# Ten feed-forward blocks by seven products, with the weight sums of two of them formed ahead and kept in DRAM

## The chip, the core and the metric

The kernel runs on one core of one Trainium2 chip. The metric is the device time of one execution in microseconds. A core has a matrix engine (TensorE, PE in the profile; its weight loads are listed as PEld), three engines for elementwise work (VectorE or DVE, ScalarE or ACT, GpSimd or POOL) and SyncE (SP), which here only issues transfers. Each engine works through its own instruction list in order and waits on semaphores. Sixteen DMA engines move data between DRAM and the core's memory; a transfer belongs to the queue of the engine that issued it. Sums of products build up in eight banks of PSUM, each 128 partitions by 512 floats.

## The reference

Two layers work on 256 tokens of width 2048, all in float32. Cut to what matters:

```python
for l in range(DEPTH):                        # 2
    h = rms_norm(x, norm1_g[l])
    z = h @ w_in[l]                           # 2048 x 3584
    mixed = ...                               # gated unit and windowed attention on parts of z
    x = x + mixed @ w_out[l]                  # 2048 x 2048
    h2 = rms_norm(x, norm2_g[l])
    x = x + (jax.nn.silu(h2 @ w_gate[l]) * (h2 @ w_up[l])) @ w_down[l]   # 2048 x 5632, 5632 x 2048
```

The change is about the last line, and about what runs beside the projections ahead of it.

## The kernel before

**Three products for one.** TensorE multiplies in a short float format (`float32r`). Each operand is split into a high part and a rest; `mm3` (lines 133 to 136) adds three matmuls: high times high, high times rest, rest times high. Activations are split once. Weights are split as they come in: `raw_load` brings a tile of 128 x 2 x 512 floats (512 KB, buffer `raw`, 7 of them) through SP's queue, and `split2` makes `wh` with a copy on ACT (line 95, 5 buffers) and `wl` with a subtraction on DVE (line 96, 4 buffers).

**A unit** is one such tile with its 12 matmuls of 128 x 512 (two halves, two groups of 128 tokens, three products). After a unit `tick()` counts a clock on, and actions entered by `later(delay, fn)` are emitted when their tick has come. In this way small steps are laid between units of matmuls in program order. The scheduler of the language then orders instructions by that order and by free buffers.

**The first part of a layer** consists of 7 blocks of 8 units (`in_block`, columns 6, 4, 5, 2, 3, 0, 1 of `w_in`), with the attention's steps placed at ticks (`UNIT_AT`), and of the output projection, 8 parts of 4 units (`add_part`). In attention DVE, ACT and POOL normalize, form the softmax and split the results; POOL computes the inverse roots (`inv_rms`, line 182, with the name `ir`) and issues the loads of the bias (line 317).

**The feed-forward part** has 11 column blocks of 512. For blocks in `GU_BLOCKS` (0 and 1), `gate_up` multiplies gate and up in the ordinary way, 16 units. For blocks in `S_BLOCKS` (2 to 10), `seven` uses a scheme like Strassen's: taking the two token groups, two interleaved halves of the depth, and the gate and up columns as 2 x 2 matrices, it needs 7 products in place of 8. A product runs through four rounds `i`, each a half-unit of 6 matmuls, so 28 half-units a block. Five PSUM banks `m0` to `m4` hold the products. In a round of the first phase DVE forms three sums of weight tiles: `b11 + b12` (line 605), that plus `b22` into `t2` (line 606), and `b12 + b22` (line 611). An accumulating transfer on POOL's queue (line 613) adds the fourth weight tile onto `t2`, which is kept for the second phase. After the first phase DVE combines the banks (lines 624 to 629); the second phase adds the products of `b21` to bank `m0` and those of the kept sums to bank `m2`, whose result DVE adds once more (line 638), and then come the SiLU on ACT (line 641) and the product with it on DVE (line 643).

**The mixture.** `s_stream` yields after each half-unit of `seven`. `std_stream` yields ordinary units: those of `gate_up`, and those of `down`, which multiplies by `w_down` two or three finished blocks at a time. Finished blocks are transposed and split by `act_T` (line 555) into tiles with the tag `aT`, of which there are 8. How many ordinary units follow a half-unit is set by `debt`, a running balance of DVE's cost (`VEC`, `VEC_P`) against PE's (`MM` times `LOAD`): ordinary units are emitted while the balance is positive. What is left runs after the last block.

Of the kernel before, what the change touches and what calls it, by code (L numbers as in the profile page):

```python
# [12 lines left out]
F32 = mybir.dt.float32  # L13
# [3 lines left out]
ALU = mybir.AluOpType  # L17
AX = mybir.AxisListType
PSUM = bass.MemoryType.PSUM

P = 128
D = 2048
SEQ = 256
NTOK = SEQ // P
# [16 lines left out]
ND = D // NB  # L41
S_BLOCKS = (2, 3, 4, 5, 6, 7, 8, 9, 10)
GU_BLOCKS = tuple(b for b in range(NFF) if b not in S_BLOCKS)
CHUNK = (2, 3)
ACT_TILES = 8
VEC = 1.14
VEC_P = 0.6
MM = 0.227
LOAD = 0.93
WARM = 12  # L50
# [14 lines left out]
def trunk(ctx, tc, x, xt, w_in, w_out, w_gate, w_up, w_down, sgu_w, sgu_g, consts,  # L65
# [7 lines left out]
    ap = ctx.enter_context(tc.tile_pool(name="ap", bufs=2))  # L73
    sp = ctx.enter_context(tc.tile_pool(name="sp", bufs=4))
    pa = ctx.enter_context(tc.tile_pool(name="pa", bufs=5, space=PSUM))
    pd = ctx.enter_context(tc.tile_pool(name="pd", bufs=2, space=PSUM))
# [12 lines left out]
    def split2(raw):  # L89
        wh = wp.tile([P, 2, NB], F32R, tag="wh", name="wh", bufs=5)  # L90
        wl = wp.tile([P, 2, NB], F32R, tag="wl", name="wl", bufs=4)
        step = 2 if clock[0] > 1 else 1
        for j in range(0, 2, step):
            src = raw[:, j : j + step, :]
            nc.scalar.copy(wh[:, j : j + step, :], src)  # L95
            nc.vector.tensor_tensor(  # L96
                wl[:, j : j + step, :], src, f(wh[:, j : j + step, :]), ALU.subtract
            )
        vec(1)
        return wh, wl  # L100

    clock = [0]
    debt = [0.0]

    def vec(n, cost=VEC):
        debt[0] += n * cost

    def pe(n):
        debt[0] -= n * MM * LOAD

    serial = itertools.count()
# [26 lines left out]
    def unit(src, acts, acc, first, last, again=False):  # L138
        raw = raw_load(src, 2 if clock[0] < 4 else 1)
        wh, wl = split2(raw)  # L140
        for j in range(2):
            act, aj = acts[j]
            for t in range(NTOK):
# [4 lines left out]
                )  # L148
        pe(12)
        tick()  # L150
# [100 lines left out]
    for lay in range(L):  # L251
# [226 lines left out]
        def norm_block(n, ss, pairs, lay, col, ext=None):  # L478
# [11 lines left out]
            for t in range(NTOK):  # L490
                sum_sq(ss[:, t, n : n + 1], xres[:, t, n * NB : (n + 1) * NB])

        acc_kv = in_block(6)
        if lay == 0:
# [55 lines left out]
        def act_T(b, c, sg, pairs_f=pairs_f):  # L550
# [4 lines left out]
            nc.vector.tensor_tensor(pair[:, 1], ps, f(pair[:, 0]), ALU.subtract)  # L555
            vec(1, VEC_P)
            pe(2)
            pairs_f.setdefault(b, []).append(pair)
# [16 lines left out]

        def seven(b, lay=lay, pairs2=pairs2, ext2=ext2, act_later=act_later):
            bank = [pa.tile([P, NB], F32, tag="acc", name=f"m{i}") for i in range(5)]

            def s_unit(raw, m, i, op, first, last, bank=bank):
                wh, wl = split2(raw)  # L580
                for j in range(2):
# [4 lines left out]
                    )  # L586
                pe(6)
                tick(0.5)
# [6 lines left out]

            kept = []
            for i in range(4):
                b11 = raw_load(w_gate[lay, b, i, 0])
                b12 = raw_load(w_up[lay, b, i, 0])
                b22 = raw_load(w_up[lay, b, i, 1])  # L600
                t2 = ap.tile([P, 2, NB], F32, tag="spt", name="t2", bufs=4)
                first, last = i == 0, i == 3
                s_unit(b11, 0, i, a_op(0, 0), first, last)
                yield
                nc.vector.tensor_tensor(b11, b11, b12, ALU.add)  # L605
                nc.vector.tensor_tensor(t2, b11, b22, ALU.add)
                s_unit(b11, 1, i, e_op(1), first, last)
                vec(1)
                vec(1)
                yield  # L610
                nc.vector.tensor_tensor(b12, b12, b22, ALU.add)
                s_unit(t2, 3, i, e_op(2), first, last)
                nc.gpsimd.dma_start(t2, w_gate[lay, b, i, 1], accum_op=ALU.add)  # L613
                vec(1)
                yield
# [8 lines left out]
            nc.scalar.copy(m0, bank[0])  # L624
            nc.vector.tensor_tensor(m0, bank[3], m0, ALU.add)
            nc.vector.tensor_tensor(c12, bank[1], m0, ALU.add)
            nc.vector.tensor_tensor(c12, bank[4], c12, ALU.add)
            nc.vector.tensor_tensor(c21, bank[2], m0, ALU.add)
            nc.vector.tensor_tensor(c22, bank[1], c21, ALU.add)
            vec(5, VEC_P)  # L630
            yield
            for i in range(4):
                b21 = raw_load(w_gate[lay, b, i, 1])
                s_unit(b21, 0, i, a_op(1, 0), False, i == 3)
                yield
                s_unit(kept[i], 2, i, a_op(1, 1), False, i == 3)
                yield
            nc.vector.tensor_tensor(m0, bank[2], m0, ALU.add)
            sg = [zp.tile([P, NB], F32, tag="z", name="sg0"), m0]
            for t, c in ((0, bank[0]), (1, m0)):  # L640
                nc.scalar.activation(sg[t], c, AF.Silu, scale=rstd2[t])
            for t, c in ((0, c12), (1, c22)):
                nc.vector.scalar_tensor_tensor(sg[t], c, nrstd2[t], sg[t], ALU.mult, ALU.mult)
            vec(3, VEC_P)
            act_later(b, sg)
# [17 lines left out]
        def gate_up(b, even=even, act_later=act_later):  # L663
# [7 lines left out]
            for t in range(NTOK):  # L671
                nc.vector.scalar_tensor_tensor(
                    sg[t], acc[t], rstd2[t], sg[t], ALU.mult, ALU.mult
                )
            vec(NTOK, VEC_P)
            act_later(b, sg)
# [49 lines left out]
        other = std_stream()  # L726
        debt[0] = 0.0
        for _ in s_stream():
            while debt[0] > 0.0 and next(other, False):
                pass  # L730
        seven_done[0] = True
# [93 lines left out]
```

## Time and profile before

| quantity | value |
|---|---|
| median of 3 runs | 1953.2 us (1952.04 to 1955.46) |
| profiled execution | 1952.96 us, span 1951.2 us |
| granted TensorE clock | 0.999 |
| PE busy | 1936.5 us, 99% |
| DVE busy | 1624.8 us, 83% |
| ACT busy | 1253.2 us, 64% |
| POOL busy | 115.3 us, 6% |
| moved by DMA | 422.2 MB, 216 GB/s on the mean |

The profile is one execution, and its busy times are unions: two instructions of an engine that overlap count once. The first 270 us are layer 0's projections, attention and output projection, the feed-forward part runs to about 900 us, and layer 1 repeats both. A matmul's duration in a row is the time from its start to its modelled end, so neighbours overlap. In rows of groups, "idle before" is how long the engine stood idle ahead of these instructions, with what ended that idling.

### The profile page before, as it was taken

How to read it: one execution, taken by the hardware profiler on the slowest of the kernel's cores; microseconds unless marked ns; L12 is line 12 of the kernel's file. 1: busy time of each engine (PE TensorE's matmuls, PEld its weight loads, DVE VectorE, ACT ScalarE, POOL GpSimd, SP SyncE). 2: the span in 40 equal slices, each digit the busy share in tenths (PEclk: the TensorE clock that was granted, in tenths of full speed). 3: DMA queues.
4: the chain of work that ended last, by engine and by line, in shares of the span. 5: the costliest groups of instructions: out<-in, count | busy, mean ns of one | idle time of the engine just before them, and what ended most of it. 6: DMA issues, size and time to landing. Idle time of an engine off the chain costs nothing.

```text
span 1951.2 us, 24946 instructions
## 1 busy us (share of the span) xinstructions
PE 1936.5 (99%) x8884; PEld 1587.5 (81%) x8884; DVE 1624.8 (83%) x1712; ACT 1253.2 (64%) x1651; POOL 115.3 (6%) x116
## 2 busy tenths in 40 slices
PE   9999999999999999999999999999999999999999
PEld 6788888888888888888887888888888888888887
DVE  6566689999999999999556656899999999999983
ACT  7565566666666666667756755666656666666674
POOL 1210000000000000000002000000000000000000
PEclk9999999999999999999999999999999999999999
DMA  9544557768678678768555355586686787778773
GB/s 358 192 146 153 189 169 227 231 225 264 214 218 268 210 229 254 226 215 262 193 200 192 132 164 181 174 256 214 214 274 205 230 253 228 221 233 247 226 252 116
DMA packets 117804, 422.20 MB, mean 216 GB/s; under 512 B 13104, under 2 KB 13744, under 8 KB 117680
## 3 DMA queue, kind: packets, MB, share of 16 engines
q1 hardware_dynamic: 105264, 375.52, 55.2%
q0 software_dynamic: 12416, 45.09, 12.8%
q8 instruction: 69, 1.13, 0.2%
q14 instruction: 55, 0.45, 0.1%
HBM read 418.47 MB, written 2.10 MB: 216 GB/s over the span
## 4 chain that ended last, share of the span: by engine, by line
PE 91%; DVE 3%; issue 3%; ACT 1%; DMA 1%; POOL 1%; SPq 0%; ACTq 0%; DVEq 0%; POOLq 0%
PE m L135 11%; PE m L136 11%; PE m L134 11%; PE dacc L135 10%; PE dacc L134 10%; PE dacc L136 10%; PE acc L135 8%; PE acc L136 8%; PE acc L134 8%; DVE wl L96 1%; PE ps_f L199 1%; POOL ir L182 1%; PE ps_v L372 1%; PE ps_n L199 1%; ACT s L349 0%
## 5 line engine op out<-in xcount | busy, mean ns | idle before, releaser
L95 ACT CAST wh<-raw 128x1024 fp32r<-128x1024 f32 (+1 forms) x778 | 800.9, 1050 | 530.4 <-DVE raw L605 173.8
L96 DVE TENSOR_TENSOR wl<-raw,wh 128x1024 fp32r<-128x1024 f32 (+1 forms) x778 | 930.4, 1218 | 171.2 <-PE acc L135 98.6
L134 PE MATMUL m<-wh,ext 128*128 128x512 f32 x576 | 226.1, 393 | 0.0
L135 PE MATMUL m<-wl,ext 128*128 128x512 f32 x576 | 224.9, 390 | 1.1 <-DVE wl L96 1.1
L135 PE MATMUL dacc<-wl,aT 128*128 128x512 f32 x576 | 225.9, 392 | 0.0
L136 PE MATMUL dacc<-wh,aT 128*128 128x512 f32 x576 | 225.0, 391 | 0.0
L136 PE MATMUL m<-wh,ext 128*128 128x512 f32 x576 | 224.8, 390 | 0.0
L134 PE MATMUL dacc<-wh,aT 128*128 128x512 f32 x576 | 224.3, 394 | 0.1
L96 DVE TENSOR_TENSOR wl<-t,wh 128x1024 fp32r<-128x1024 f32 x144 | 175.8, 1221 | 28.0 <-PE dacc L135 10.4
L134 PE MATMUL acc<-wh,hT 128*128 128x512 f32 x448 | 179.7, 403 | 1.1 <-ACT wh L95 1.1
L135 PE MATMUL acc<-wl,hT 128*128 128x512 f32 x448 | 176.3, 394 | 1.2 <-DVE wl L96 1.2
L136 PE MATMUL acc<-wh,hT 128*128 128x512 f32 x448 | 175.9, 393 | 0.0
L95 ACT CAST wh<-t 128x1024 fp32r<-128x1024 f32 x144 | 151.2, 1050 | 36.9 <-PE dacc L136 21.9
L134 PE MATMUL m<-wh,hT 128*128 128x512 f32 x432 | 168.4, 390 | 0.0
L136 PE MATMUL m<-wh,hT 128*128 128x512 f32 x432 | 168.3, 389 | 0.0
L135 PE MATMUL m<-wl,hT 128*128 128x512 f32 x432 | 168.3, 389 | 0.0
L134 PE MATMUL acc<-wh,aT 128*128 128x512 f32 x384 | 151.5, 395 | 0.0
L136 PE MATMUL acc<-wh,aT 128*128 128x512 f32 x384 | 150.1, 391 | 0.0
L135 PE MATMUL acc<-wl,aT 128*128 128x512 f32 x384 | 149.7, 390 | 0.0
L613 POOL DMA_DIRECT2D t<-in_w_gate_dram x72 | 61.6, 856 | 1321.3 <-DVE wl L96 1113.1
L135 PEld LDWEIGHTS dacc<-wl,aT 128*128 128x128 f32 x576 | 108.2, 188 | 26.4 <-DVE wl L96 4.7
L134 PEld LDWEIGHTS dacc<-wh,aT 128*128 128x128 f32 x576 | 107.8, 188 | 25.2 <-ACT dacc L686 2.0
(138 smaller groups left out, 2839.4 us busy)
## 6 DMA issues: line engine op xcount, KB each, us to landing
raw<-in_w_gate_dram SPq DMA_DIRECT2D x176, 512.0 KB, 6.0
raw<-in_w_up_dram SPq DMA_DIRECT2D x176, 512.0 KB, 4.4
raw<-in_w_down_dram SPq DMA_DIRECT2D x176, 512.0 KB, 4.8
raw<-in_w_in_dram SPq DMA_DIRECT2D x108, 512.0 KB, 4.3
t<-in_w_gate_dram POOLq DMA_DIRECT2D x72, 512.0 KB, 7.0
raw<-in_w_out_dram SPq DMA_DIRECT2D x64, 512.0 KB, 3.4
bias<-in_band_dram POOLq DMA_DIRECT2D x8, 512.0 KB, 4.5
xr<-in_xt_dram SPq DMA_DIRECT2D x8, 256.0 KB, 6.7
```

Of the source, the lines that this page charges most:

```text
L95: nc.scalar.copy(wh[:, j : j + step, :], src)
L96: nc.vector.tensor_tensor(wl[:, j : j + step, :], src, f(wh[:, j : j + step, :]), ALU.subtract)
L134: nc.tensor.matmul(acc, ah, wh, start=first, stop=False, skip_group_check=again)
L135: nc.tensor.matmul(acc, ah, wl, start=False, stop=False, skip_group_check=again)
L136: nc.tensor.matmul(acc, al, wh, start=False, stop=last, skip_group_check=again)
L182: anchor[0] = nc.gpsimd.tensor_tensor(r, ms, mhalf[:, :n], ALU.pow)
L199: nc.tensor.transpose(ps[:, j, t * P : (t + 1) * P], blocks[t][:, j * P : (j + 1) * P], ident)
L372: nc.tensor.matmul(pv[:, r, i], pt[:, (r * n + i) * (t + 1) + b, :], zkv[b][:, cols], start=b == 0, stop=b == t,)
L613: nc.gpsimd.dma_start(t2, w_gate[lay, b, i, 1], accum_op=ALU.add)
```

## The change

`S_BLOCKS` becomes 1 to 10, so that ten blocks go by seven products and block 0 alone is ordinary. Four things go with it.

- The sums of blocks 1 and 2 (`PRE`) are formed ahead. `presum` is entered at ticks 18, 21 and so on to 39 of a layer's projections, once for each of two blocks and four rounds. It loads three weight tiles through SP's queue into tiles with the tag `aT`, forms the three sums on DVE and stores them through POOL's queue into a pool in DRAM. In `seven` these blocks load the stored sums in place of forming them; the fourth weight tile is added onto the kept sum by DVE in the second phase, instead of by the accumulating transfer.
- Bank `m2` is combined first, and ACT copies the combination back into the bank, so that the second phase accumulates onto it and the later addition goes. In the second phase the two products are shifted against one another by one round.
- The running balance is replaced by an even spread: after step `k` of the 300 steps of `s_stream`, ordinary units are emitted while `done * 300 < (k + 1) * 88`. Of the 104 ordinary units, 16 (`TAIL`) are left for the end.
- The products with SiLU's output use the tiles `m0` and `c21` again.

```diff
--- before.py
+++ after.py
@@ -17,6 +17,7 @@
 ALU = mybir.AluOpType
 AX = mybir.AxisListType
 PSUM = bass.MemoryType.PSUM
+DRAM = bass.MemoryType.DRAM
 
 P = 128
 D = 2048
@@ -39,14 +40,14 @@
 NI = 3584 // NB
 NFF = DFF // NB
 ND = D // NB
-S_BLOCKS = (2, 3, 4, 5, 6, 7, 8, 9, 10)
+S_BLOCKS = (1, 2, 3, 4, 5, 6, 7, 8, 9, 10)
 GU_BLOCKS = tuple(b for b in range(NFF) if b not in S_BLOCKS)
 CHUNK = (2, 3)
 ACT_TILES = 8
-VEC = 1.14
-VEC_P = 0.6
-MM = 0.227
-LOAD = 0.93
+HALVES = 30 * len(S_BLOCKS)
+STD_UNITS = 8 * NFF + 16 * len(GU_BLOCKS)
+TAIL = 16
+PRE = S_BLOCKS[:2]
 WARM = 12
 UNIT_AT = (6, 9, 12, 15, 19, 23)
 
@@ -72,6 +73,7 @@
     zp = ctx.enter_context(tc.tile_pool(name="zp", bufs=8))
     ap = ctx.enter_context(tc.tile_pool(name="ap", bufs=2))
     sp = ctx.enter_context(tc.tile_pool(name="sp", bufs=4))
+    dp = ctx.enter_context(tc.tile_pool(name="dp", bufs=1, space=DRAM))
     pa = ctx.enter_context(tc.tile_pool(name="pa", bufs=5, space=PSUM))
     pd = ctx.enter_context(tc.tile_pool(name="pd", bufs=2, space=PSUM))
     pm = ctx.enter_context(tc.tile_pool(name="pm", bufs=1, space=PSUM))
@@ -96,18 +98,9 @@
             nc.vector.tensor_tensor(
                 wl[:, j : j + step, :], src, f(wh[:, j : j + step, :]), ALU.subtract
             )
-        vec(1)
         return wh, wl
 
     clock = [0]
-    debt = [0.0]
-
-    def vec(n, cost=VEC):
-        debt[0] += n * cost
-
-    def pe(n):
-        debt[0] -= n * MM * LOAD
-
     serial = itertools.count()
     pending = []
 
@@ -146,7 +139,6 @@
                     acc[t], act[:, 0, aj, ts], act[:, 1, aj, ts], wh[:, j, :], wl[:, j, :],
                     first and j == 0, last and j == 1, again,
                 )
-        pe(12)
         tick()
 
     def product(srcs, pairs):
@@ -489,6 +481,23 @@
                 later(2 + c, lambda c=c: to_T(c))
             for t in range(NTOK):
                 sum_sq(ss[:, t, n : n + 1], xres[:, t, n * NB : (n + 1) * NB])
+
+        sums = {}
+
+        def presum(b, i, lay=lay, sums=sums):
+            keep = dp.tile([3, P, 2, NB], F32, tag=f"sum{lay}_{b}_{i}", name="sums")
+            t = []
+            for w, q in ((w_gate, 0), (w_up, 0), (w_up, 1)):
+                x = tp.tile([P, 2, NB], F32, tag="aT", name="pre")
+                nc.sync.dma_start(x, w[lay, b, i, q])
+                t.append(x)
+            for k in range(3):
+                nc.vector.tensor_tensor(t[k], t[k], t[(k + 1) % 3], ALU.add)
+                nc.gpsimd.dma_start(keep[k], t[k])
+            sums[b, i] = keep
+
+        for k, (b, i) in enumerate(itertools.product(PRE, range(4))):
+            later(18 + 3 * k, lambda b=b, i=i: presum(b, i))
 
         acc_kv = in_block(6)
         if lay == 0:
@@ -553,8 +562,6 @@
             pair = tp.tile([P, 2, 2, SEQ], F32R, tag="aT", name="aT")
             nc.scalar.copy(pair[:, 0], ps)
             nc.vector.tensor_tensor(pair[:, 1], ps, f(pair[:, 0]), ALU.subtract)
-            vec(1, VEC_P)
-            pe(2)
             pairs_f.setdefault(b, []).append(pair)
 
         held = []
@@ -573,7 +580,7 @@
 
                 later(2 + c, ready)
 
-        def seven(b, lay=lay, pairs2=pairs2, ext2=ext2, act_later=act_later):
+        def seven(b, lay=lay, pairs2=pairs2, ext2=ext2, act_later=act_later, sums=sums):
             bank = [pa.tile([P, NB], F32, tag="acc", name=f"m{i}") for i in range(5)]
 
             def s_unit(raw, m, i, op, first, last, bank=bank):
@@ -584,7 +591,6 @@
                         bank[m], ah, al, wh[:, j, :], wl[:, j, :], first and j == 0,
                         last and j == 1, m in (0, 2),
                     )
-                pe(6)
                 tick(0.5)
 
             def a_op(k, t):
@@ -594,24 +600,31 @@
                 return lambda p, h: ext2[p][:, h, n, :]
 
             kept = []
+            pre = b in PRE
             for i in range(4):
                 b11 = raw_load(w_gate[lay, b, i, 0])
-                b12 = raw_load(w_up[lay, b, i, 0])
+                t2 = ap.tile([P, 2, NB], F32, tag="spt", name="t2", bufs=4)
+                if pre:
+                    s1 = raw_load(sums[b, i][0])
+                    nc.sync.dma_start(t2, sums[b, i][2])
+                    b12 = raw_load(sums[b, i][1])
+                else:
+                    b12 = raw_load(w_up[lay, b, i, 0])
                 b22 = raw_load(w_up[lay, b, i, 1])
-                t2 = ap.tile([P, 2, NB], F32, tag="spt", name="t2", bufs=4)
                 first, last = i == 0, i == 3
                 s_unit(b11, 0, i, a_op(0, 0), first, last)
                 yield
-                nc.vector.tensor_tensor(b11, b11, b12, ALU.add)
-                nc.vector.tensor_tensor(t2, b11, b22, ALU.add)
-                s_unit(b11, 1, i, e_op(1), first, last)
-                vec(1)
-                vec(1)
+                if not pre:
+                    s1 = b11
+                    nc.vector.tensor_tensor(s1, b11, b12, ALU.add)
+                    nc.vector.tensor_tensor(t2, s1, b22, ALU.add)
+                s_unit(s1, 1, i, e_op(1), first, last)
                 yield
-                nc.vector.tensor_tensor(b12, b12, b22, ALU.add)
+                if not pre:
+                    nc.vector.tensor_tensor(b12, b12, b22, ALU.add)
                 s_unit(t2, 3, i, e_op(2), first, last)
-                nc.gpsimd.dma_start(t2, w_gate[lay, b, i, 1], accum_op=ALU.add)
-                vec(1)
+                if not pre:
+                    nc.gpsimd.dma_start(t2, w_gate[lay, b, i, 1], accum_op=ALU.add)
                 yield
                 s_unit(b22, 4, i, e_op(3), first, last)
                 yield
@@ -623,25 +636,27 @@
             )
             nc.scalar.copy(m0, bank[0])
             nc.vector.tensor_tensor(m0, bank[3], m0, ALU.add)
+            nc.vector.tensor_tensor(c21, bank[2], m0, ALU.add)
+            nc.scalar.copy(bank[2], c21)
             nc.vector.tensor_tensor(c12, bank[1], m0, ALU.add)
+            nc.vector.tensor_tensor(c22, bank[1], c21, ALU.add)
             nc.vector.tensor_tensor(c12, bank[4], c12, ALU.add)
-            nc.vector.tensor_tensor(c21, bank[2], m0, ALU.add)
-            nc.vector.tensor_tensor(c22, bank[1], c21, ALU.add)
-            vec(5, VEC_P)
             yield
-            for i in range(4):
-                b21 = raw_load(w_gate[lay, b, i, 1])
-                s_unit(b21, 0, i, a_op(1, 0), False, i == 3)
-                yield
-                s_unit(kept[i], 2, i, a_op(1, 1), False, i == 3)
-                yield
-            nc.vector.tensor_tensor(m0, bank[2], m0, ALU.add)
-            sg = [zp.tile([P, NB], F32, tag="z", name="sg0"), m0]
-            for t, c in ((0, bank[0]), (1, m0)):
+            for i in range(5):
+                if i < 4:
+                    b21 = raw_load(w_gate[lay, b, i, 1])
+                    s_unit(b21, 0, i, a_op(1, 0), False, i == 3)
+                    yield
+                    if pre:
+                        nc.vector.tensor_tensor(kept[i], kept[i], b21, ALU.add)
+                if i > 0:
+                    s_unit(kept[i - 1], 2, i - 1, a_op(1, 1), False, i == 4)
+                    yield
+            sg = [m0, c21]
+            for t, c in ((0, bank[0]), (1, bank[2])):
                 nc.scalar.activation(sg[t], c, AF.Silu, scale=rstd2[t])
             for t, c in ((0, c12), (1, c22)):
                 nc.vector.scalar_tensor_tensor(sg[t], c, nrstd2[t], sg[t], ALU.mult, ALU.mult)
-            vec(3, VEC_P)
             act_later(b, sg)
             yield
 
@@ -672,7 +687,6 @@
                 nc.vector.scalar_tensor_tensor(
                     sg[t], acc[t], rstd2[t], sg[t], ALU.mult, ALU.mult
                 )
-            vec(NTOK, VEC_P)
             act_later(b, sg)
 
         left = [NFF]
@@ -724,10 +738,10 @@
                     yield False
 
         other = std_stream()
-        debt[0] = 0.0
-        for _ in s_stream():
-            while debt[0] > 0.0 and next(other, False):
-                pass
+        done = 0
+        for k, _ in enumerate(s_stream()):
+            while done * HALVES < (k + 1) * (STD_UNITS - TAIL) and next(other, False):
+                done += 1
         seven_done[0] = True
         for went in other:
             if not went:
```

In all there are 8644 matmul instructions instead of 8692, 40 more transfers issued by POOL and 80 more by SP.

## The prediction

> **What bounds the kernel now.** I read first the page's busy times, its slices and its chain of waits, then stretches of the span by engine.
>
> ```profile
> span 1951.2 us, 24946 instructions
> PE 1936.5 (99%) x8884; PEld 1587.5 (81%) x8884; DVE 1624.8 (83%) x1712; ACT 1253.2 (64%) x1651; POOL 115.3 (6%) x116
> DVE  6566689999999999999556656899999999999983
> PE 91%; DVE 3%; issue 3%; ACT 1%; DMA 1%; POOL 1%; SPq 0%; ACTq 0%; DVEq 0%; POOLq 0%
> 300.00:900.00 600.00, 599.29 (x2667) 491.93 (x2666) 570.64 (x534) 391.86 (x440) 29.88 (x35) 1.00 0.76 234
> ```
>
> PE is busy for 99% of the span and 91% of the chain. DVE's 83% is a mean of two stages: sixes in attention, nines in the feed-forward part. The last row is that part in layer 0 (columns: window, PE, weight loads, DVE, ACT, POOL, clock, DMA share, GB/s): PE lacks 0.7 of 600 us, DVE is busy for 570.6, 95%. So PE bounds, with DVE 5% behind it, and only fewer matmuls or fewer stalls save time. What a matmul costs is its distance to the next, not its 0.39 us of latency:
>
> ```profile
> 504.08 0.39 PE L134 MATMUL m<-wh,hT 128*128 128x512 f32 x1
> 504.31 0.39 PE L135 MATMUL m<-wl,hT 128*128 128x512 f32 x1
> 504.54 0.39 PE L136 MATMUL m<-wh,hT 128*128 128x512 f32 x1
> 504.76 0.39 PE L134 MATMUL m<-wh,hT 128*128 128x512 f32 x1
> ```
>
> Three distances in 0.68 us: 0.227 us each.
>
> **Fewer matmuls.** An ordinary gate and up block takes 16 units of 12 matmuls, 192; one by seven products takes 28 half-units of 6, 168. One block in each layer changes kind: 2 x 24 x 0.227 = **-10.9 us**. It is also the most that the change can give: PE lacks 0.7 us in the 600 shown, and no gap elsewhere is addressed.
>
> **DVE in the feed-forward part.** The prices:
>
> ```profile
> L96 DVE TENSOR_TENSOR wl<-t,wh 128x1024 fp32r<-128x1024 f32 x144 | 175.8, 1221 | 28.0 <-PE dacc L135 10.4 <-PE m L135 6.9 <-issue 6.2
> L605 DVE TENSOR_TENSOR raw<-raw 128x1024 f32<-128x1024 f32 x72 | 88.2, 1225 | 2.3
> L611 DVE TENSOR_TENSOR raw<-raw 128x1024 f32<-128x1024 f32 x72 | 87.7, 1218 | 0.0
> L555 DVE TENSOR_TENSOR aT<-ps_f,aT 128x512 fp32r<-128x512 f32 x44 | 30.2, 686 | 7.5 <-ACT aT L554 7.3
> L643 DVE SCALAR_TENSOR_TENSOR m<-c,nr,m 128x512 f32<-128x512 f32 x18 | 13.4, 745 | 0.0
> L638 DVE TENSOR_TENSOR m<-m,m 128x512 f32<-128x512 f32 x18 | 12.3, 683 | 0.0
> 512.23 1.22 DVE L96 TENSOR_TENSOR wl<-t,wh 128x1024 fp32r<-128x1024 f32 x1
> 513.36 4.62 DVE L96 TENSOR_TENSOR wl<-raw,wh 128x1024 fp32r<-128x1024 f32 x4
> ```
>
> A split or sum of 128x1024 lasts 1.22 us, but four in a row end after 4.62: 3 distances and one latency, so 1.13 us each, and 512.23 to 513.36 says the same. For PSUM operands I take the same 0.93 of the duration: about 0.64 and 0.69 us.
>
> Before, nine blocks with 11 to 12 ordinary units each: PE 168 + 138 matmuls, 69.5 us; DVE 28 splits, 12 sums and 11.5 splits by 1.13, six PSUM combinations, two L643 and two L555, 64.7 us; 93%, and 95% with the gaps it has. After, 104 - 16 = 88 ordinary units are dealt over ten blocks, 9 to a block: PE 276 matmuls, 62.7 us, and about 0.8 for the transposes, 63.5. DVE in the eight blocks a layer that still form their sums: 49 x 1.13 + 5 x 0.64 + 2 x 0.69 + 2 x 0.64 = 61.2 us. With the first block's sums left out, the two blocks that read stored sums are easier: 8 operations less (12 sums become 4), 9 us. So DVE stands at 96 to 97% in 16 blocks. Within such a block it is tighter: of 30 steps five belong to each first-phase round, which gets 1.47 ordinary units; PE has 30 + 17.6 matmuls, 10.8 us, and DVE 8 + 1.47 operations, 10.7 us. Four rounds in a row run at 99%; the slack lies in the second phase. What gaps DVE has that are not spare time:
>
> ```profile
> DVE wl L96 <- PE dacc L135: 8.3, 16, 1.5
> DVE wl L96 <- issue: 4.0, 5, 1.3
> DVE aT L555 <- ACT aT L554: 3.1, 6, 0.6
> DVE wl L96 <- ACT wh L95: 2.0, 6, 0.6
> ```
>
> These are the DVE waits of 300 to 900 us. The first is a wait for PE to give a buffer back, so it is slack. The last two, 5.1 us over 600 / 69.5 = 8.6 blocks, are 0.6 us a block of late ACT work. A round has 0.1 to spare, so 0.6 a block is partly passed on; four wl buffers take some of it. Bounds: nothing if the second phase gives the lead back in time, 0.6 x 16 = 9.6 us if every such gap reaches PE. I take 0.25 a block, nearer to the lower end since PE lost 0.7 us in 600 before: **+4 us**.
>
> **The rest of the block.** The accumulating DMA goes in the blocks with stored sums, 72 to 64 in all; nothing on the chain waited for it, so nothing is gained. In every block m2's second phase now waits for one DVE addition and one ACT copy into the bank: 0.68 (L638 above) and 0.58,
> ```profile
> L624 ACT COPY m<-m 128x512 f32<-128x512 f32 x18 | 10.4, 577 | 0.0
> ```
>
> about 2 us with hand-overs. Between the last first-phase matmul on that bank and the first second-phase one lay 30 matmuls before, 6.8 us, and lie 24 now in most blocks and 19 in the least, 4.3 us: hidden, cost nothing; if DVE is then 2.3 us behind, what is left over is paid per block. One DVE combination less is in the sum above. ACT gains 78 copies on an engine that was busy for 391.9 of 600 us: nothing.
>
> **The presums.** In each layer eight groups of 3 loads on SP's queue, 3 DVE adds and 3 stores on POOL's.
>
> ```profile
> 50.00:165.00 115.00, 111.22 (x612) 91.55 (x611) 71.25 (x112) 73.50 (x150) 19.06 (x12) 1.00 0.47 155
> 20.00:30.00 10.00, 10.00 (x44) 7.95 (x43) 6.01 (x7) 8.99 (x18) 0.00 (x0) 1.00 1.03 412
> L613 POOL DMA_DIRECT2D t<-in_w_gate_dram x72 | 61.6, 856 | 1321.3 <-DVE wl L96 1113.1
> DVE v L428 <- POOL ir L182: 6.1, 2, 3.1
> DVE wl L96 <- PE acc L135: 14.2, 9, 2.4
> PE ps_p L363 <- ACT s L349: 2.3, 1, 2.3
> PE ps_v L372 <- DVE aT L190: 0.9, 1, 0.9
> ```
>
> 24 adds by 1.13 are 27 us a layer; DVE has 44 of 115 us free between 50 and 165 us, but of its waits there only 14.2 us (fifth row) are lead, a split waiting for PE. PE itself waits there 0.9 us for an attention result of DVE's (last row). An add put ahead of such a result delays it by up to its 1.22 us, a group by 3.7; bounds 0 and 8 x 1.22 = 10. I take one add reaching PE in each layer: **+2.4 us**. POOL: a store issue is like L613's, 0.86 us; three queued ahead of the power operation `ir`, for which DVE waits 3.1 us at most, would add 2.6 to that wait; DVE's lead covers it once, so it is in the same term.
>
> Transfers: at full rate a 512 KB tile takes 0.524 / 0.412 = 1.27 us. In layer 0 a group brings six transfers to the three of the units beside it: 9 x 1.27 = 11.4 us. How long three units last there:
>
> ```profile
> raw<-in_w_in_dram SPq DMA_DIRECT2D x29, 512.0 KB, 4.2
> ```
>
> 29 loads in 50 to 165 us, so 11.9 us for three: just covered. In layer 1 the instruction order puts six of the eight groups ahead, at the end of layer 0's feed-forward part and in the first projections: one extra load and one store per unit for some 18 units, 3 x 1.27 = 3.8 us against 2.72, 20 us in all. Seven raw buffers hold 7 x 2.72 = 19 us of work. Bounds: 0 and 20; I take what exceeds the buffers, **+1.2 us**.
>
> The Trainium skill ("DMA: Bandwidth & Descriptors", Specifications) gives a limit of about 358 GB/s from HBM per core, 1.46 us a tile, by which the shortfall would be 18 x (4.39 - 2.72) - 19 = 11 us, an estimate. The trace ran at 412 GB/s for 10 us, so it speaks against that for reads; no row shows stores beside them.
>
> **Sum**, against the profiled execution's 1952.96 us (its span is 1951.2; the median of the runs is 1953.2, 0.2 above): -10.9 + 4 + 2.4 + 1.2 = -3.3, so **1949.7 us**. About 0.2%, 3.9 us, is what measurement can tell from no change, and the forecast lies just inside it.
>
> **Rivals.** *PE keeps its lead*: the gaps fall into the second phase and the presums into DVE's spare time. For it: 14.2 us of lead, DVE under 97%. Then -10.9 + 0 to 4: 1942 to 1946.
>
> *DVE becomes the bound* (slower side): in the 16 blocks the reserve is 63.5 - 61.2 = 2.3 us, 3.6%. Before, 570.6 us were busy where 8.6 blocks of 64.7 make 556, so operations stood 3% wider than back to back, 1.16 us; so a block needs 61.2 x 1.03 + 0.6 us of gaps = 63.6, and each further 0.02 us in that distance costs 16 x 49 x 0.02 = 16 us. At 1.18 it is 16 x 1.1 = 18 for these blocks, -10.9 + 18 + 3.6 = +10.7, 1963.6. It decides once DVE needs over 63.5 us. Against it: distances of 1.13 when nothing waits, and the 3% may be ends of runs, where spare time follows.
>
> *No overlap at all*: at 1.22 a block needs 66.1, 16 x 2.6 = 42 us, so 1984. The Trainium skill states such a rule ("VectorE: DVE Perf Modes", The DRAIN you can't avoid): the next operation does not start until the pipe has emptied. The trace disagrees: four in 4.62 us, not 4.88.
>
> *Transfers bound the change of layers*: the stores slow the loads, or the loads queued ahead in SP's queue hold up weights; half of the 20 us and 5 in layer 0 give -3.3 + 14 = 1964. For it: the order hoists the groups, so those sums are not formed during attention as intended; one load waiting for a buffer or a store holds all weights behind it. Against: a DMA share of 0.47 in attention.
>
> **Chances.** Forecast (1946 to 1953) 0.38; PE keeps its lead 0.27; DVE the bound 0.19; no overlap 0.02; transfers 0.14. Faster than -0.2% is all of the second and 0.13 of the forecast; slower is 0.17, 0.02 and 0.13 of the last three and 0.06 of the forecast; the rest, 0.22, is the same. The range of 1942 to 1966 leaves out no overlap, the far halves of the two slow rivals, and little below.
>
> **What would show it.** Matmuls fewer by 48. PE idle in the feed-forward window of 600 us: 2 us if right; over 6 means DVE bounds, and DVE would then be busy for 98% or more, with PE waiting for L96. At the end of layer 0's feed-forward part and in layer 1's first projections: DMA share near 1.0 and PE waits of a few us if right; over 8 means transfers. Waits of PE on the second-phase products after the copy into the bank would refute the zero put there. The prediction is wrong if PE's gaps grow by under 4 or over 11 us.

## The result and the profile after

The changed kernel takes 1968.8 us (median of 4 runs, 1966.5 to 1972.9) against 1953.4 for the kernel before: 15.4 us slower, a ratio of 1.008 with a 95% interval of 1.0068 to 1.0093. That lies beyond the range of 1942 to 1966. The profiled execution took 1966.54 us.

The page of the changed kernel:

```profile
span 1964.7 us, 25338 instructions
PE 1935.3 (99%) x8836; PEld 1581.8 (81%) x8836; DVE 1675.1 (85%) x1768; ACT 1315.7 (67%) x1733; POOL 133.2 (7%) x156
DMA  9977557867777787678996675578577677877783
HBM read 456.21 MB, written 27.26 MB: 246 GB/s over the span
```

PE has 48 instructions fewer, as counted. Its busy time fell by only 1.2 us, because a busy time of overlapping matmuls also counts those that run slowly. The DMA row has two new hills: its first slices, and those about 930 to 1030 us. Both are where the stored sums are formed: in layer 0's projections, and at the change of layers.

By stretches (columns: window, PE, weight loads, DVE, ACT, POOL, clock, DMA share, GB/s), first before, then after:

```profile
50.00:150.00 100.00, 96.22 (x534) 78.79 (x533) 61.72 (x96) 63.40 (x135) 16.12 (x11) 1.00 0.49 165
270.00:900.00 630.00, 629.29 (x2806) 516.76 (x2805) 596.05 (x571) 410.49 (x469) 31.56 (x37) 1.00 0.75 231
900.00:1050.00 150.00, 150.00 (x697) 122.79 (x696) 91.08 (x103) 98.46 (x152) 8.44 (x7) 1.00 0.63 210
```

```profile
50.00:150.00 100.00, 93.97 (x479) 75.48 (x479) 76.61 (x105) 59.26 (x124) 27.64 (x31) 0.95 0.91 362
270.00:900.00 630.00, 627.82 (x2800) 514.97 (x2799) 591.96 (x573) 435.98 (x505) 26.36 (x31) 1.00 0.74 237
900.00:1050.00 150.00, 141.65 (x636) 115.53 (x635) 111.61 (x119) 97.18 (x138) 19.89 (x27) 0.99 0.91 326
```

In the 100 us from 50 on, PE executes 479 instructions instead of 534, at a DMA share of 0.91 instead of 0.49. From 900 on it is idle for 8.4 us where it had no gap. The feed-forward window hardly differs.

A finer measure is PE's gaps: over successive matmuls, the part of the start-to-start distance beyond 0.227 us (a float32 matmul of 128x512; for all others 0.110), where it exceeds 0.06 us, summed over a stretch.

| PE gaps, us | 0-50 | 50-270 | 270-900 | 900-1270 | 1270-1890 | after | all |
|---|---|---|---|---|---|---|---|
| before | 7.1 | 11.6 | 6.0 | 12.7 | 5.7 | 0.2 | 43.2 |
| changed | 6.3 | 21.4 | 6.9 | 24.5 | 7.0 | 0.2 | 66.1 |
| no stored sums | 5.9 | 11.5 | 7.6 | 12.8 | 9.0 | 0.2 | 47.0 |
| no stored sums, first block alone | 6.9 | 13.0 | 6.4 | 13.2 | 6.3 | 0.4 | 46.1 |

The changed kernel's gaps grew by 22.9 us, 21.6 of them in the two stretches of projections. 22.9 - 10.9 = 12.0 of the 13.6 us between the two profiled executions. Not all of it is waiting: matmuls at a lower granted clock count too. The clock of 0.95 and 0.99 in the changed kernel's rows, against 1.00 before, makes 0.05 x 100 + 0.01 x 150 = 6.5 us, an estimate; the last section has the rows for it.

### The profile page after: what moved, and what is told of

The parts are those of the page before. It is cut to its first block, busy times and chain, and to the rows that moved or that the text cites. A ratio compares the mean times of both kernels' runs of the same rounds, so it can differ in the third digit from the quotient of the medians.

```text
span 1964.7 us, 25338 instructions
## 1 busy us (share of the span) xinstructions
PE 1935.3 (99%) x8836; PEld 1581.8 (81%) x8836; DVE 1675.1 (85%) x1768; ACT 1315.7 (67%) x1733; POOL 133.2 (7%) x156
## 4 chain that ended last, share of the span: by engine, by line
PE 88%; DVE 4%; issue 4%; ACT 1%; DMA 1%; POOL 1%; SPq 0%; ACTq 0%; DVEq 0%; POOLq 0%
PE m L128 13%; PE m L127 12%; PE m L129 12%; PE dacc L127 8%; PE dacc L128 8%; PE dacc L129 8%; PE acc L128 8%; PE acc L129 8%; PE acc L127 8%; DVE wl L98 2%; DMA pre<-in_w_up_dram 1%; PE ps_f L191 1%; PE ps_v L364 1%; ACT wh L97 1%; PE ps_n L191 1%
## 5 line engine op out<-in xcount | busy, mean ns | idle before, releaser
L97 ACT CAST wh<-raw 128x1024 fp32r<-128x1024 f32 (+1 forms) x786 | 806.6, 1050 | 422.0 <-PE acc L129 132.4
L98 DVE TENSOR_TENSOR wl<-raw,wh 128x1024 fp32r<-128x1024 f32 (+1 forms) x786 | 935.1, 1219 | 146.2 <-PE acc L128 63.4
L128 PE MATMUL m<-wl,ext 128*128 128x512 f32 x640 | 251.4, 393 | 1.6 <-DVE wl L98 1.5
L127 PE MATMUL m<-wh,ext 128*128 128x512 f32 x640 | 251.6, 394 | 1.3 <-ACT wh L97 1.0
L129 PE MATMUL m<-wh,ext 128*128 128x512 f32 x640 | 249.7, 390 | 0.0
L98 DVE TENSOR_TENSOR wl<-t,wh 128x1024 fp32r<-128x1024 f32 x160 | 194.6, 1220 | 2.7 <-issue 1.3
L97 ACT CAST wh<-t 128x1024 fp32r<-128x1024 f32 x160 | 168.5, 1053 | 37.6 <-PE m L129 18.1
L128 PE MATMUL m<-wl,hT 128*128 128x512 f32 x480 | 187.4, 390 | 1.5 <-DVE wl L98 1.5
L129 PE MATMUL m<-wh,hT 128*128 128x512 f32 x480 | 187.2, 390 | 0.0
L127 PE MATMUL m<-wh,hT 128*128 128x512 f32 x480 | 186.0, 390 | 0.0
L128 PEld LDWEIGHTS m<-wl,ext 128*128 128x128 f32 x640 | 120.2, 188 | 31.8 <-DVE wl L98 7.7
L127 PEld LDWEIGHTS m<-wh,ext 128*128 128x128 f32 x640 | 120.2, 188 | 26.9 <-ACT wh L97 2.6
L129 PEld LDWEIGHTS m<-wh,ext 128*128 128x128 f32 x640 | 120.2, 188 | 24.2
```

Of the source, the lines that this page charges most:

```text
L98: nc.vector.tensor_tensor(wl[:, j : j + step, :], src, f(wh[:, j : j + step, :]), ALU.subtract)
L127: nc.tensor.matmul(acc, ah, wh, start=first, stop=False, skip_group_check=again)
L128: nc.tensor.matmul(acc, ah, wl, start=False, stop=False, skip_group_check=again)
L129: nc.tensor.matmul(acc, al, wh, start=False, stop=last, skip_group_check=again)
```

## Experiments

### Where the loss lies

**No stored sums.** Only `PRE = ()`.

> The changed kernel with no sums formed ahead: all ten blocks form their three sums in DVE and use the accumulating transfer. Transfer theory (the loss lies in the projections, where the stored sums' loads and stores fill the DMA engines and the in-order queues pass the delay on; in the trace PE's gaps there grew by 21 us, in the feed-forward part by 2): all of the 21 us goes, the 10.9 us of fewer matmuls stay, 1943 to 1947 us. DVE theory (at 96 to 97% DVE holds PE up in blocks that form their sums, and the stored sums relieve two blocks a layer): no better than the changed kernel, 1965 us or more.

It took 1950.1 us, ratio 0.998 (0.9972 to 0.9989): faster than the kernel before, and 18.7 us faster than the changed kernel. So stored sums were the loss, and ten blocks by seven products were a gain. It missed the transfer theory's 1943 to 1947 by 3 us: the table shows 4.9 us of new gaps in the feed-forward parts, which come up again below.

**Stored sums alone.** The kernel before, with `presum` and its calls for two blocks and no reader.

> The kernel before with the sums of two blocks a layer formed ahead and stored at the same ticks, and never read; the feed-forward part stays as it was. Transfer theory: it costs what the projections lost in the changed kernel, 21 us of gaps and some clock, 1972 to 1978 us. DVE theory: the projections hide it, 1953 to 1958 us.

It took 1975.3 us, 22.4 more than before, as the transfer theory had it. Its windows:

```profile
50.00:150.00 100.00, 92.20 (x468) 73.87 (x466) 76.19 (x105) 57.14 (x121) 27.30 (x31) 0.93 0.89 356
270.00:900.00 630.00, 629.41 (x2808) 517.57 (x2807) 594.03 (x574) 407.49 (x465) 30.64 (x36) 1.00 0.74 229
960.00:1050.00 90.00, 80.93 (x354) 65.99 (x353) 59.30 (x67) 49.27 (x79) 13.38 (x21) 0.94 0.96 358
```

The feed-forward part is untouched; both projections show the changed kernel's picture, with a granted clock of 0.93 and 0.94.

**Stored sums in layer 0 alone.**

```diff
-for k, (b, i) in enumerate(itertools.product(PRE, range(4))):
+for k, (b, i) in enumerate(itertools.product(PRE if lay == 0 else (), range(4))):
-pre = b in PRE
+pre = lay == 0 and b in PRE
```

> The changed kernel with stored sums in layer 0 alone; layer 1 forms its sums in the blocks. In the changed kernel PE's gaps between 960 and 1270 us are 12 us longer than before. If the loss is made in each layer by its own sums: 1955 to 1959 us. Rival, the two layers' losses are not separate, or layer 1's blocks pay for their sums in DVE: 1962 us or more.

1958.7 us: 8.6 above the kernel without stored sums, 10.1 below the one with them in both layers. The two losses are separate, and about equal.

**Half of it.** `PRE = S_BLOCKS[:1]`, groups at ticks 18, 24, 30, 36.

> The changed kernel with stored sums for one block a layer and its four groups at twice the distance, so half the traffic and half the additions, spread over the same ticks. If the loss comes from the DMA engines being full, it falls by far more than half, as their share comes below 0.85: 1949 to 1954 us. If each addition and transfer has its price, it is halfway between the kernels with and without stored sums: 1958 to 1961 us.

1953.0 us. Half the sums cost 2.9 us of the 18.7, not 9. The stretch of layer 0 in which the changed kernel ran at full share, in the changed kernel and then here, and after it the change of layers here:

```profile
40.00:130.00 90.00, 88.45 (x455) 70.75 (x454) 66.53 (x86) 53.05 (x109) 26.92 (x29) 0.98 1.03 415
40.00:130.00 90.00, 87.33 (x459) 70.91 (x457) 62.73 (x87) 55.05 (x112) 22.09 (x20) 0.98 0.78 298
960.00:1000.00 40.00, 34.95 (x161) 27.83 (x161) 27.44 (x35) 26.71 (x49) 4.99 (x9) 0.96 0.91 328
PE ps_n L191 <- DVE hT L182: 5.1, 2, 3.7
```

So there is no fixed price per transfer. In layer 0, at a share of 0.78, little is lost: PE's gaps from 50 to 270 us are 13.3 us, against 11.5 without stored sums. At the change of layers they are 19.7 against 12.8, with waits of PE for `hT` that come up below, although the share from 960 to 1050 us is only 0.74: it is 0.91 in the first 40 us. The 2.9 us also contain a gain, 2.3 us less of gaps in the feed-forward parts.

### What passes the delay on

From 40 to 140 us the issues (line, count, size, median us to landing), before and after:

```profile
raw<-in_w_in_dram SPq DMA_DIRECT2D x28, 512.0 KB, 4.3
wm<-in_sgu_w_dram POOLq DMA_DIRECT2D x2, 512.0 KB, 4.2
```

```profile
raw<-in_w_in_dram SPq DMA_DIRECT2D x22, 512.0 KB, 12.7
sums<-pre POOLq DMA_DIRECT2D x18, 512.0 KB, 9.6
wm<-in_sgu_w_dram POOLq DMA_DIRECT2D x2, 512.0 KB, 11.5
```

These transfers land after 10 to 13 us instead of 4. That is harmless for a weight tile issued early, and not for one that an in-order queue waits for. The changed kernel's timelines of POOL, DVE and PE in layer 0 show the chain:

```profile
127.23 1.09 POOL L392 TENSOR_SCALAR_AFFINE_SELECT wm<-wm 128x1024 f32<-128x1024 f32 x1 [12.38 <-DMA wm<-in_sgu_w_dram]
128.29 2.92 POOL L174 TENSOR_TENSOR ir<-ms,mhalf 128x16 f32<-128x16 f32 x1
```

```profile
124.45 0.17 DVE L172 TENSOR_SCALAR ms<-hs 128x16 f32<-128x16 f32 x1
131.25 1.29 DVE L420 TENSOR_TENSOR v<-v,ir 128x512 f32<-128x512 f32 x2 [6.63 <-POOL ir L174]
133.66 0.87 DVE L182 SCALAR_TENSOR_TENSOR aT<-ps_t,cst,aT 128x256 fp32r<-128x256 f32 x2
```

```profile
PE ps_v L364 <- DVE aT L182: 4.5, 1, 4.5
```

POOL waits 12.4 us for the gated unit's weights `wm` to mask them. The inverse root `ir`, whose input was ready at 124.6, stands behind that and ends at 131.2; DVE waits for it 6.6 us with the split `aT` behind, and PE waits 4.5 us for that.

**No mask.** The changed kernel without the affine selections on `wm`.

> The changed kernel without GpSimd's masking of the gated unit's weights (the two affine selections a layer are left out, so the upper triangle isn't zeroed). In the changed kernel's trace POOL waits 12.4 us in layer 0 for these weights' load, and the power operation for which DVE and then PE wait stands behind it. If this queue is what passes the full DMA engines on to PE in layer 0, PE's gap of 4.6 us near 131 us goes and the time falls by 4 to 7 us, to 1962 to 1965. Rival, the weight tiles themselves are late: no change, 1967 to 1970.

1960.8 us, 8.0 less and so more than the 4 to 7 expected, though the share from 40 to 130 us is still full:

```profile
40.00:130.00 90.00, 87.34 (x456) 69.90 (x455) 68.53 (x90) 53.27 (x109) 25.46 (x27) 1.00 1.03 415
PE ps_v L364 <- DVE aT L182: 0.9, 1, 0.9
```

PE's gaps from 50 to 270 us fall from 21.4 to 15.4. The wait for `aT` is 0.9 us, as in the kernel before, so it accounts for 3.6 of that. The clock, 1.00 from 50 to 150 us instead of 0.95, accounts for about 5, an estimate; other waits grew by some 3.

**The same with stored sums in layer 0 alone.**

> The same with stored sums in layer 0 alone, and without GpSimd's masking in both layers (the two affine selections a layer are left out). If nearly all of layer 0's loss goes by the mask's wait in POOL's queue: 7 to 9 us below the kernel with stored sums in layer 0 alone, 1948 to 1951 us. Rival, it is a common delay by full DMA engines: 2 to 4 us below, 1953 to 1956.

1952.2 us, 6.5 less than with the masks. The expected 7 to 9 was missed by half a microsecond. Of layer 0's 8.6 us some 2.1 are left, if the masks cost nothing in the kernel without stored sums, which was not run without them. So the wait in POOL's queue, with the lower clock behind it, is most of layer 0's loss.

In layer 1, six of the eight groups are loaded ahead of their ticks, from 944 to 1018 us, across the change of layers. The changed kernel's waits from 900 to 1060 us, of DVE and of PE:

```profile
DVE pre L495 <- DMA pre<-in_w_up_dram: 18.9, 10, 4.9
```

```profile
PE ps_n L191 <- DVE hT L182: 8.3, 4, 3.3
```

DVE stands ten times at an addition whose tile has not landed, with the split of the layer's own normalized input `hT` behind it, for which PE waits.

**Additions four ticks later.** The additions and stores of a group go into a function of their own, entered by `later(4, add)`.

> The changed kernel with each group's additions and stores entered 4 ticks after its loads, so that DVE should not stand waiting for a load; the traffic is the same. If DVE's in-order queue, held by an addition whose tile has not landed (18.9 us of such waits at the change of layers), is what passes the delay on, PE's 10 us of gaps there go: 1957 to 1962 us. Rival, the full DMA engines delay the weights in any order: 1966 to 1970 us.

1964.5 us, between the two, so neither expectation held. What fell is layer 0's (gaps of 18.2 us from 50 to 270 us instead of 21.4). At the change of layers DVE still waited 17.9 us for such tiles and PE's gaps stayed (24.4 us): the additions again followed their loads too closely. It doesn't tell the theories apart.

**No additions.**

> The changed kernel without the 24 additions a layer on DVE in the projections; loads and stores stay, so what is stored are the weights themselves and not their sums. Transfer theory: the DMA engines stay full and most of the loss stays, 1960 to 1969 us. Rival, the additions standing in DVE's queue ahead of attention's results are the loss: 1944 to 1950 us.

1955.8 us. 13.0 of the 18.7 us go, though the transfers stay. In the window of layer 0 the traffic is fuller than ever, and PE loses little:

```profile
50.00:150.00 100.00, 96.11 (x515) 77.45 (x514) 59.22 (x92) 61.67 (x125) 26.44 (x32) 0.98 1.02 407
```

PE's waits for `hT` at the change of layers are gone as well. What stands there instead is a wait behind POOL's queue, for the keys `k`:

```profile
PE ps_t L191 <- DVE k L268: 3.5, 1, 3.5
DVE k L268 <- POOL ir L174: 12.5, 1, 12.5
```

`ir` stands behind eight stores there, each of which waits 2.1 to 3.9 us for the load of its tile. The transfer theory in its plain form (full engines delay the weights) expected 1960 to 1969 and is too simple; so is the rival, at 1944 to 1950.

**No stores.** The additions stay, the blocks read weights where they read sums.

> The changed kernel without the stores: loads and additions stay, and the feed-forward part loads weights in place of the sums, as many bytes. Transfer theory: the projections' traffic falls by a third of a group's nine transfers, DMA share under 0.9, most of the loss goes: 1946 to 1954 us. Rival, the additions are the loss: 1963 us or more.

1951.3 us, as the transfer theory had it: 17.5 of 18.7 go. With a third less traffic in a group, the share from 50 to 150 us is 0.76 instead of 0.91. Removing either half takes off most of the loss, and 13.0 + 17.5 is more than the whole. So the two act together: transfers near the limit, whose time to landing doubles or triples, and an instruction in an in-order queue (an addition on DVE, the mask or a store on POOL) that waits for one of them with attention's results behind it.

A third queue was held up too, SP's, in the changed kernel:

```profile
SPq L492 <- DMA sums<-pre: 33.3, 12, 7.2
```

A load of `presum` waits there until a store has landed and freed one of the eight tiles `aT`, with the weight loads behind it; all twelve waits lie in layer 0. No run takes this wait away alone: it is 3.6 us without the additions, and gone without the stores. But without the mask it is still 30.6 us, while PE's wait in layer 0 is back at 0.9, so that run's gain did not come from it.

### The feed-forward part

**A hole in the mixture.** The 4.9 us of new gaps without stored sums sit near 325 and 415 us, and alike in layer 1. `gate_up` has given its 16 units by step 55, and `down` wants two finished blocks, which it gets only after step 60. For five steps there is no ordinary unit, so DVE's heavy rounds stand alone.

```diff
-if len(full) >= CHUNK[0] or rest:
+if len(full) >= CHUNK[0] or rest or (full and not gus and not downed):
```

> The kernel without stored sums, in which the down projection may begin with one finished block alone as soon as block 0's gate and up are done. Without this the stream of ordinary units is empty from step 56 to step 61 of each layer, two units short, and PE's gaps near 415 and 1385 us are 3.1 and 4.4 us. Hole theory: these gaps go, 4 to 6 us below the kernel without stored sums, 1944 to 1946 us. DVE theory (DVE holds PE up in any block that forms its sums): 1949 to 1952 us.

1944.6 us, ratio 0.9951 (0.9939 to 0.9964): 5.5 less than without this line, as expected. Part of that is the clock: 0.999 to 1.000 in its runs, 0.996 to 0.999 without the line. Its feed-forward row has PE full and DVE at 97%:

```profile
270.00:900.00 630.00, 629.29 (x2801) 514.32 (x2800) 611.23 (x590) 440.16 (x518) 34.10 (x40) 1.00 0.75 233
```

**The same line in the changed kernel.**

> The changed kernel, in which the down projection may begin with one finished block alone. If the hole in the stream of ordinary units costs it what it cost the kernel without stored sums (5.5 us): 1962 to 1964 us. Rival, with stored sums DVE has the reserve to cover the hole: 1967 to 1970 us.

1968.1 us, no gain. The hole is gone there too (gaps from 270 to 900 us fall from 6.9 to 4.9, from 1270 on from 7.0 to 5.8), but those from 900 to 1270 rise from 24.5 to 29.2. In this execution 17 us of that stretch ran at half clock instead of 3.4, which by estimate (half of the difference) is 6.8 us, more than the rise. So why the gain doesn't appear stays open beyond that; four runs of each kernel, with clocks of 0.993 to 0.997, do not separate it.

**The old second phase.** Without stored sums and with that line, but bank `m2` starts empty, the two products are not shifted, and DVE adds bank `m2` once more at the end.

> The kernel without stored sums and with the first block alone in the down projection, with the second phase as it was before the change: bank m2 starts empty and DVE adds it once more at the end, one DVE operation of 0.68 us a block more. By the prediction's zero for the addition and the copy ahead of the second phase, and DVE at 97%: within 2 us, 1943 to 1947 us. Rival, the copy into the bank holds PE up and undoing it gains: 1940 to 1942 us; or the further DVE operation is too much: 1949 us or more.

1956.0 us, 11.4 more. The prediction had put this part of the change at nothing, beside 0.64 us of DVE time a block. Three more runs ask for the reason.

**One more DVE operation**, after the combinations:

```diff
 nc.vector.tensor_tensor(c12, bank[4], c12, ALU.add)
+nc.vector.tensor_tensor(m0, c12, c22, ALU.add)
```

> The kernel without stored sums and with the first block alone, and one further DVE addition of 128x512 a block after the combinations, which nothing needs (it lands in a tile that is written over later). If DVE's capacity is what the old second phase exceeded: 20 x 0.6 = 10 to 12 us more, 1953 to 1957 us. If it was the order of the second phase: within 2 us, 1943 to 1947 us.

1946.5 us: 1.9 us more by the medians, 3.7 by the ratios to each one's own runs of the kernel before (0.9970 against 0.9951). That is far from 11.4, so the count of DVE's operations is not the main reason.

**Fewer ordinary units in a block.** `TAIL = 24`.

> The kernel without stored sums and with the first block alone, with 24 ordinary units a layer left for the end in place of 16, so 8 instead of 9 in a block. By the durations PE needs 60.8 us a block and DVE 60.1. If DVE's ceiling is near 96% of PE's time, as one more DVE operation a block costing 11.4 us suggests: 20 x (60.1 / 0.964 - 60.8) = 31 us more, 1970 to 1978 us. If DVE can go to 99% beside PE, no change: 1943 to 1948 us.

1943.3 us, ratio 0.9955 (0.9941 to 0.9968), within the noise the same. No loss, and DVE goes to 98.7%:

```profile
270.00:900.00 630.00, 627.92 (x2802) 515.72 (x2801) 621.65 (x603) 448.25 (x522) 35.00 (x41) 1.00 0.74 237
```

My expected 31 us took 96% for a ceiling, and fell.

**The two halves of the second phase.** First the old addition in the new order of products, then the new copy in the old order.

> The kernel without stored sums and with the first block alone (1944.6 us); bank m2 starts empty and DVE adds it once more at the end of the block, as before the change, but the two products of the second phase keep the change's order, shifted by one round. One DVE operation a block costs nothing after the combinations, so if its place decides (at the end of a block it stands in DVE's queue in the next block's first rounds, where DVE has no gap): 1952 to 1957 us. If the order of the products made the 11.4 us: 1943 to 1947 us.

> The same kernel with the copy into bank m2 as changed and the products in the order from before, without the shift, so 19 matmuls and not 24 between the last first-phase product on m2 and the first that needs the copy at the least. If the place of the DVE operation decides: 1943 to 1947 us. If the order decides: 1952 to 1957 us, and PE's gaps would stand at the first product on m2 in the second phase.

1955.2 and 1947.2 us: with the old addition 10.6 us more, with the old order 2.5 more, which is hardly clear of the noise. In the first of them, DVE's timeline at the start of a block:

```profile
676.25 1.22 DVE L619 TENSOR_TENSOR raw<-raw 128x1024 f32<-128x1024 f32 x1
677.50 1.23 DVE L620 TENSOR_TENSOR t<-raw 128x1024 f32<-128x1024 f32 x1
678.64 0.68 DVE L654 TENSOR_TENSOR m<-m,m 128x512 f32<-128x512 f32 x1
679.24 1.22 DVE L98 TENSOR_TENSOR wl<-raw,wh 128x1024 fp32r<-128x1024 f32 x1
```

The addition ending a block (L654) runs within the next block's first round, between its sums (L619, L620) and its splits (L98). From there on DVE's timeline shows no gap for some 40 us. 10.6 / 20 blocks = 0.53 us, nearly the operation's 0.60 to the next start, and PE's gaps in the feed-forward parts are 22.7 us instead of 12.7. The further operation of the earlier run ended the first phase and cost 2 to 4 us. So the place of an operation in DVE's queue is the likeliest reason, but it is not shown alone: this run also drops ACT's copy and lets a SiLU wait for the addition. Where PE's larger waits lie, they are mostly for ACT's `wh`, and these copies in turn wait for DVE's sums, first in the version with the copy into the bank (1944.6 us), then here (270 to 900 us):

```profile
ACT wh L97 <- DVE raw L619: 81.2, 32, 4.4
ACT wh L97 <- DVE raw L619: 89.9, 33, 4.5
```

## Why the prediction was wrong

- **Fewer matmuls, -10.9 us: right.** 48 instructions fewer; with nothing else in the way the gain is about 9 us (1944.6 and 1943.3, each against its own runs of the kernel before).
- **DVE in the feed-forward part, +4 us: wrong in place.** The blocks run without loss at 97% and even at 98.7%. What the part loses (2.2 us of gaps in the changed kernel, 4.9 without stored sums) is a hole in the stream of ordinary units, which the count per block, 9, hid. The mean of 9 was never checked against when blocks are ready. The forecast sign, 2 us of idle PE in the feed-forward window, came true (2.2 of 630 us in the changed kernel), but for another reason than ACT's late work.
- **The rest of the block, nothing: the copy hides, but the part is worth 10.6 to 11.4 us** in the kernel without stored sums. I priced the removed addition by its 0.64 us as one of 61, though the prediction itself had found the first-phase rounds at 99%: what an operation costs seems to depend on where it stands in DVE's queue.
- **The presums, 2.4 + 1.2 us: the step that failed.** They cost 18.7 us (22.4 in the kernel before). For layer 0 I compared throughput (11.4 us of transfers in 11.9) and called it covered. It ran at the limit for 90 us, and the time to landing tripled. I listed what stands behind a store on POOL and priced three store issues, 2.6 us, but not that the mask ahead of `ir` would wait for a load: 12.4 us. An addition was priced by its 1.22 us, not by the wait for its tile with the splits behind it: 18.9 us of such waits of DVE, and 8.3 us of PE's for `hT`, at the change of layers. The 1.2 us for what exceeds the seven buffers is about 0.6 by the prediction's own figures (18 x 1.09 - 19.0).
- **The rivals.** *Transfers bound the change of layers*, with a chance of 0.14 and 1964 us, came nearest: it had the hoisted groups and a load that holds others behind it. Its sign came too: PE lost 8.4 us from 900 to 1050 us, over the 8 named. It gave layer 0 only half the change of layers, while the losses are 8.6 and 10.1 us, and it looked for late weights, while the weights were hardly what PE waited for; the load that holds the weights behind it did happen, in layer 0 (33.3 us on SP's queue). *DVE becomes the bound* did not decide: with DVE at 98.7% PE is busy for 627.9 of 630 us. *No overlap at all* is refuted in the same stretch, where the durations of DVE's 602 operations add up to 665.8 us.
- **The limit of about 358 GB/s** ("DMA: Bandwidth & Descriptors", Specifications, in the Trainium skill): the trace disagrees with stores in the mix too, 415 GB/s over 90 us (40 to 130 us).

## What to carry to other kernels

Transfers moved into a quiet stretch are not free once the DMA engines come near full: everything lands late, so look in each in-order queue for an instruction that waits for a load and for what stands behind it, and price the time to landing beside the throughput. A mean share can hide it: with half the sums it was 0.74 over 90 us at the change of layers, and PE still waited 5.1 us. Where an engine is nearly full in one phase and free in another, the price of an operation can depend on its place: here 2 to 4 us in one, 10.6 in the other. A mean rate between two streams of work says nothing of whether both have work at each step. The version that came out of this drops the stored sums, keeps the rest, and lets the second stream begin earlier: 1944.6 us, and with 24 units kept for the end 1943.3, the same within the noise.

## What the runs showed of the hardware

After a stall TensorE can run at half rate for a few microseconds. In the changed kernel a gap of 3.5 us ends at 1001.6 us. The matmuls run at full rate for 1.4 us more and then slow down, while the granted clock falls to 0.5:

```profile
1002.51 0.39 PE L127 MATMUL acc<-wh,hT 128*128 128x512 f32 x1
1002.74 0.44 PE L128 MATMUL acc<-wl,hT 128*128 128x512 f32 x1
1002.98 0.63 PE L129 MATMUL acc<-wh,hT 128*128 128x512 f32 x1
1003.40 0.63 PE L127 MATMUL acc<-wh,hT 128*128 128x512 f32 x1
1003.83 0.63 PE L128 MATMUL acc<-wl,hT 128*128 128x512 f32 x1
1004.26 0.63 PE L129 MATMUL acc<-wh,hT 128*128 128x512 f32 x1
1003.00:1006.00 3.00, 3.00 (x9) 2.35 (x8) 1.31 (x3) 0.48 (x1) 0.53 (x1) 0.50 1.06 393
81.00:85.00 4.00, 4.00 (x15) 3.08 (x15) 3.81 (x7) 2.42 (x10) 1.06 (x2) 0.57 1.04 421
136.00:143.00 7.00, 6.73 (x29) 6.29 (x29) 4.68 (x9) 5.32 (x12) 0.60 (x1) 0.52 0.00 0
```

The distance is 0.43 us instead of 0.227 for eight matmuls, so this stall is paid for with some 1.6 us more. The Trainium skill ("TensorE: Matmul & The Clock Gate", Part 1) describes such a gate, which lets half the pulses through when TensorE has been little busy; the trace agrees with the half. The last two rows are the other stretches of the changed kernel at half clock, one behind the wait for `aT` of 4.5 us. Together the three last 13.6 us, which cost 6.8 us by estimate; the kernel before and the run without the mask had none ahead of their last microseconds, the stored sums alone had 27.3 us of them. How long a gap must be is not shown: the stretch at 81 us followed a gap of only 1.0 us, while one of 2.5 us at 90 us in the kernel before had none behind it. The runs of the changed kernel follow the clock roughly: 1966.5 us at a mean of 0.997, 1968.0 at 0.995, 1969.5 at 0.993, 1972.9 at 0.994.
